# Softmax cross entropy on one core: labels' logits by a masked sum on VectorE instead of by gathers

## Chip, cores, metric

One core of one Trainium2 chip. The metric is device time in microseconds (us) of one execution; lower is better. All runs told of here are fast, with a granted clock of 1.00. When two kernels are compared as a ratio, it is the mean time of one kernel's fast runs over that of the other's fast runs of the same rounds, so it is not quite the ratio of the medians quoted beside it.

## The reference

```python
batch, seq, vocab = 16, 512, 32000        # logits float32, labels int
logits_max = np.max(logits, axis=-1, keepdims=True)
log_sum_exp = np.log(np.sum(np.exp(logits - logits_max), axis=-1)) + logits_max.squeeze(-1)
log_probs = logits - log_sum_exp[..., np.newaxis]
loss = -log_probs[np.arange(batch)[:, None], np.arange(seq), labels]
```

There are 8192 rows of 32000 logits, 1048.6 MB, each read once. A row needs the sum of its exponentials and one single element, its label's logit.

## The kernel before

The rows are laid over 128 partitions in 64 groups (`G`). A group is read in two loads of 16000 columns (8.19 MB each) into three buffers of 64 KB per partition. ScalarE takes exp in place and sums it in the same call (`accum_out`; the trace has one activation of 13.54 us and one accumulator read of 0.19 us for each). The labels' logits come from 64 gathers that GpSimd issues at the start, each fetching 128 single elements.

```python
    nc.gpsimd.iota(idx[:], pattern=[[V, G]], base=0, channel_multiplier=G * V)
    nc.gpsimd.tensor_tensor(out=idx[:], in0=idx[:], in1=labs32, op=ALU.add)
    for g in range(G):
        nc.gpsimd.indirect_dma_start(
            out=lab_logit[:, g:g + 1], out_offset=None, in_=lg,
            in_offset=bass.IndirectOffsetOnAxis(ap=idx[:, g:g + 1], axis=1),
        )
    # ...
    for j, (g, b, at, n) in enumerate(loads):
        if b not in buffers:
            buffers[b] = data.tile([P, W], FP32, tag="t", name="t")     # 3 buffers, W = 16000
        t = buffers[b]
        # ...
        nc.sync.dma_start(out=t[:, at:at + n], in_=lg_pg[:, g, c0:c0 + n])
        exp(g, t[:, at:at + n])          # one activation with accum_out
        # ... at the end: log of the sums, minus lab_logit, two small stores
```

The softmax here doesn't subtract the row's maximum and nothing guards it: scores larger than these inputs give would overflow.

Of the kernel before, what the change touches and what calls it, by code (L numbers as in the profile page):

```python
# [1 line left out]

# [5 lines left out]

FP32 = mybir.dt.float32  # L10
I32 = mybir.dt.int32


EXP = mybir.ActivationFunctionType.Exp
LN = mybir.ActivationFunctionType.Ln
ALU = mybir.AluOpType
X = mybir.AxisListType.X


@with_exitstack  # L20
def kernel(
    ctx: ExitStack,
    tc: tile.TileContext,
    logits: bass.AP,
    labels: bass.AP,
    out: bass.AP,
):
    nc = tc.nc

    B, S, V = logits.shape  # L30
    P = 128
    G = B * S // P
    W = 16000


    lg = logits.rearrange("b s v -> (b s) v")
    lg_pg = lg.rearrange("(p g) v -> p g v", g=G)
    labels_pg = labels.rearrange("b s -> (b s)").rearrange("(p g) -> p g", g=G)
    out_pg = out.rearrange("b s -> (b s)").rearrange("(p g) -> p g", g=G)



    loads = []

    def plan(g, widths_by_buffer, order):

        n_buffers = 1 + max((l[1] for l in loads), default=-1)
        for b, i in order:
            ws = widths_by_buffer[b]
            loads.append((g, n_buffers + b, sum(ws[:i]), ws[i]))  # L50

    plan(0, [[4000, 4000, 8000], [16000]], [(0, 0), (0, 1), (0, 2), (1, 0)])
    for g in range(1, G - 2):
        plan(g, [[W], [W]], [(0, 0), (1, 0)])
    plan(G - 2, [[W], [10000, 6000]], [(0, 0), (1, 0), (1, 1)])
    plan(
        G - 1,
        [[7400, 5840, 2260], [4540, 3720, 2920, 1780, 1460, 1120], [960]],
        [(0, 0), (0, 1), (1, 0), (1, 1), (1, 2), (0, 2), (1, 3), (1, 4), (1, 5), (2, 0)],
    )  # L60
    assert sum(l[3] for l in loads) == G * V

    data = ctx.enter_context(tc.tile_pool(name="data", bufs=3))
    persist = ctx.enter_context(tc.tile_pool(name="persist", bufs=1))

    labs64 = persist.tile([P, G], mybir.dt.int64)
    labs32 = labs64[:].bitcast(I32).rearrange("p (g two) -> p g two", two=2)[:, :, 0]
    idx = persist.tile([P, G], I32)
    lab_logit = persist.tile([P, G], FP32)
    K = 10  # L70
    sums = persist.tile([P, G - 1, 5], FP32)
    sums_last = persist.tile([P, K], FP32)
    totals = persist.tile([P, G - 1], FP32)
    logsum = persist.tile([P, G - 1], FP32)
    res = persist.tile([P, G - 1], FP32)
    part = persist.tile([P, 1], FP32)
    logsum_last = persist.tile([P, 1], FP32)
    res_last = persist.tile([P, 1], FP32)

    ctx.enter_context(tc.manual_schedule())  # L80


    nc.scalar.dma_start(out=labs64[:], in_=labels_pg)
    nc.scalar.preload_act_table_set("natural_log_exp_and_others")  # L84
    nc.vector.memset(sums[:], 0.0)  # L85
    nc.gpsimd.iota(idx[:], pattern=[[V, G]], base=0, channel_multiplier=G * V)  # L86
    nc.gpsimd.tensor_tensor(out=idx[:], in0=idx[:], in1=labs32, op=ALU.add)  # L87
    for g in range(G):
        nc.gpsimd.indirect_dma_start(  # L89
            out=lab_logit[:, g:g + 1],  # L90
            out_offset=None,
            in_=lg,
            in_offset=bass.IndirectOffsetOnAxis(ap=idx[:, g:g + 1], axis=1),
        )


    buffers = {}
    col = {}
    n_exp = {}

    def exp(g, ap):
        k = n_exp.get(g, 0)
        n_exp[g] = k + 1
        s = sums[:, g, k:k + 1] if g < G - 1 else sums_last[:, k:k + 1]
        nc.scalar.activation(out=ap, in_=ap, func=EXP, accum_out=s)  # L105

    for j, (g, b, at, n) in enumerate(loads):
        if b not in buffers:
            buffers[b] = data.tile([P, W], FP32, tag="t", name="t")
        t = buffers[b]  # L110
        c0 = col.get(g, 0)
        col[g] = c0 + n
        nc.sync.dma_start(out=t[:, at:at + n], in_=lg_pg[:, g, c0:c0 + n])  # L113
        exp(g, t[:, at:at + n])

        left = len(loads) - 1 - j
        if left == 6:
            nc.vector.reduce_sum(out=totals[:], in_=sums[:], axis=X)  # L118
        if left == 4:
            nc.scalar.activation(out=logsum[:], in_=totals[:], func=LN)  # L120
            nc.vector.tensor_tensor(out=res[:], in0=logsum[:], in1=lab_logit[:, 0:G - 1], op=ALU.subtract)  # L121
        if left == 1:
            nc.vector.reduce_sum(out=part[:], in_=sums_last[:, 0:K - 1], axis=X)  # L123
    assert n_exp[G - 1] == K
    nc.sync.dma_start(out=out_pg[:, 0:G - 1], in_=res[:])

    nc.scalar.activation(out=logsum_last[:], in_=sums_last[:, K - 1:K], func=LN, bias=part[:])  # L127
    nc.vector.tensor_tensor(out=res_last[:], in0=logsum_last[:], in1=lab_logit[:, G - 1:G], op=ALU.subtract)  # L128
    nc.sync.dma_start(out=out_pg[:, G - 1:G], in_=res_last[:])


# [1 line left out]
_INS = ['logits', 'labels']  # L133
_OUTS = [((16, 512), 'float32')]


# [23 lines left out]
```

## Time and profile before

| | before |
|---|---|
| time, median of 3 runs | 2435.72 us (2435.60 to 2435.73) |
| span in the profile | 2434.1 us |
| DMA rate over the span | 431 GB/s |
| ScalarE / VectorE busy | 72% / 0% |
| time between landings of two full loads, from 300 us on | 18.90 us |

These lines are from the page of the kernel before: the span, the busy time of each engine, the rate in 40 slices, the DMA queues (q1 carries the 1048.62 MB of the loads, q0 the gathers), the chain of work that ended last, two groups of instructions (busy us, mean ns | idle before) and the time from a load's issue to its landing.

```profile
span 2434.1 us, 807 instructions
...
DVE 1.3 (0%) x5; ACT 1748.9 (72%) x281; POOL 61.0 (3%) x70
...
GB/s 421 422 421 433 425 438 431 427 438 438 433 426 436 438 434 426 435 438 434 426 435 436 435 430 431 436 435 430 431 436 438 431 427 436 438 433 426 438 433 377
...
q1 hardware_dynamic: 20304, 1048.62, 99.8%
q0 software_dynamic: 2048, 0.04, 0.1%
...
q14 instruction: 6, 0.05, 0.0%
...
DMA t<-in_logits_dram 76%; ACT t L105 24%; SPq L113 0%; ACTq L105 0%; ACT logsum_last L127 0%; DVE res_last L128 0%; ACT logsum L120 0%
...
L105 ACT ACTIVATE t<-t 128x16000 f32<-128x16000 f32 (+5 forms) x139 | 1734.8, 12481 | 681.4 <-DMA t<-in_logits_dram 681.2
L89 POOL DMA_INDIRECT lab_logit<-in_logits_dram,idx x64 | 60.3, 942 | 178.3 <-DMA lab_logit<-in_logits_dram,idx 174.5
...
t<-in_logits_dram SPq DMA_DIRECT2D x124, 8000.0 KB, 43.0
```

The kernel is bound by its loads. ScalarE waits for landings (681 us in all); an exp holds up only the issue of a later load. The 24% of exp in the chain is not lost time: a load is issued when the exp three loads earlier frees its buffer (SyncE waits 2330.9 us for exps, 125 times), and its 43.0 us to the landing are 2.3 times the 18.90 us between landings, so it lies queued behind two others for most of them.

The windows of the kernel before (window, its length, busy time of VectorE, ScalarE and GpSimd with instruction counts, clock, DMA share, GB/s) show where the rate is lower:

```profile
60.00:120.00 60.00, 0.00 (x0) 41.67 (x7) 13.15 (x14) 1.00 1.01 427
...
180.00:240.00 60.00, 0.00 (x0) 43.35 (x7) 13.14 (x14) 1.00 1.01 427
...
600.00:1200.00 600.00, 0.00 (x0) 430.90 (x64) 0.00 (x0) 1.00 1.00 434
```

While GpSimd issues gathers, the loads run at 427 GB/s; afterwards at 434.

### The profile page before, as it was taken

How to read it: one execution, taken by the hardware profiler on the slowest of the kernel's cores; microseconds unless marked ns; L12 is line 12 of the kernel's file. 1: busy time of each engine (PE TensorE's matmuls, PEld its weight loads, DVE VectorE, ACT ScalarE, POOL GpSimd, SP SyncE). 2: the span in 40 equal slices, each digit the busy share in tenths (PEclk: the TensorE clock that was granted, in tenths of full speed). 3: DMA queues.
4: the chain of work that ended last, by engine and by line, in shares of the span. 5: the costliest groups of instructions: out<-in, count | busy, mean ns of one | idle time of the engine just before them, and what ended most of it. 6: DMA issues, size and time to landing. Idle time of an engine off the chain costs nothing.

```text
span 2434.1 us, 807 instructions
## 1 busy us (share of the span) xinstructions
DVE 1.3 (0%) x5; ACT 1748.9 (72%) x281; POOL 61.0 (3%) x70
## 2 busy tenths in 40 slices
DVE  0000000000000000000000000000000000000000
ACT  4777766777677776777677776777667776777769
POOL 3222000000000000000000000000000000000000
DMA  9999999999999999999999999999999999999998
GB/s 421 422 421 433 425 438 431 427 438 438 433 426 436 438 434 426 435 438 434 426 435 436 435 430 431 436 435 430 431 436 438 431 427 436 438 433 426 438 433 377
DMA packets 22502, 1048.77 MB, mean 431 GB/s; under 512 B 4576, under 2 KB 4704, under 8 KB 5216
## 3 DMA queue, kind: packets, MB, share of 16 engines
q1 hardware_dynamic: 20304, 1048.62, 99.8%
q0 software_dynamic: 2048, 0.04, 0.1%
q10 hardware_dynamic: 144, 0.07, 0.0%
q14 instruction: 6, 0.05, 0.0%
HBM read 1048.67 MB, written 0.03 MB: 431 GB/s over the span
## 4 chain that ended last, share of the span: by engine, by line
DMA 76%; ACT 24%; issue 0%; SPq 0%; ACTq 0%; DVE 0%
DMA t<-in_logits_dram 76%; ACT t L105 24%; SPq L113 0%; ACTq L105 0%; ACT logsum_last L127 0%; DVE res_last L128 0%; ACT logsum L120 0%
## 5 line engine op out<-in xcount | busy, mean ns | idle before, releaser
L105 ACT ACTIVATE t<-t 128x16000 f32<-128x16000 f32 (+5 forms) x139 | 1734.8, 12481 | 681.4 <-DMA t<-in_logits_dram 681.2
L89 POOL DMA_INDIRECT lab_logit<-in_logits_dram,idx x64 | 60.3, 942 | 178.3 <-DMA lab_logit<-in_logits_dram,idx 174.5
L105 ACT ACTIVATION_READ_ACCUMULATOR t<-t 128x1 f32 x139 | 25.9, 186 | 0.0
L84 ACT ACT_TABLE_LOAD x1 | 1.3, 1283 | 1.2 <-PEq L144 1.2
L118 DVE TENSOR_REDUCE totals<-sums 128x63 f32<-128x315 f32 x1 | 0.5, 480 | 2398.9 <-ACT t L105 2398.9
L87 POOL TENSOR_TENSOR idx<-idx,labs 128x64 int32<-128x64 int32 x1 | 0.3, 322 | 7.5 <-DMA labs<-in_labels_dram 7.5
L85 DVE MEMSET sums<- 128x315 f32 x1 | 0.3, 321 | 0.9 <-PEq L144 0.9
L127 ACT ACTIVATE logsum_last<-sums_last,part 128x1 f32<-128x1 f32 x1 | 0.3, 294 | 0.0
L121 DVE TENSOR_TENSOR res<-logsum,lab_logit 128x63 f32<-128x63 f32 x1 | 0.2, 225 | 25.3 <-ACT logsum L120 25.3
L120 ACT ACTIVATE logsum<-totals 128x63 f32<-128x63 f32 x1 | 0.2, 238 | 0.0
L86 POOL IOTA idx<- 128x64 int32 x1 | 0.2, 172 | 0.4 <-PEq L155 0.4
L123 DVE TENSOR_REDUCE part<-sums_last 128x1 f32<-128x9 f32 x1 | 0.2, 163 | 4.0 <-ACT t L105 4.0
L128 DVE TENSOR_TENSOR res_last<-logsum_last,lab_logit 128x1 f32<-128x1 f32 x1 | 0.2, 159 | 1.2 <-ACT logsum_last L127 1.2
L144 POOL MEMSET const-uint8-127<- 128x1 uint8 x1 | 0.1, 118 | 0.0
L144 POOL MEMSET const-bfloat16-1.0<- 128x1 bf16 x1 | 0.1, 113 | 0.0
L144 POOL MEMSET const-float32-0.0<- 128x1 f32 x1 | 0.1, 98 | 0.2 <-issue 0.2
L144 POOL MEMSET const-float32-1.0<- 128x1 f32 x1 | 0.1, 104 | 0.0
## 6 DMA issues: line engine op xcount, KB each, us to landing
t<-in_logits_dram SPq DMA_DIRECT2D x124, 8000.0 KB, 43.0
t<-in_logits_dram SPq DMA_DIRECT2D x1, 5000.0 KB, 35.9
t<-in_logits_dram SPq DMA_DIRECT2D x2, 2000.0 KB, 9.6
t<-in_logits_dram SPq DMA_DIRECT2D x1, 4000.0 KB, 21.4
t<-in_logits_dram SPq DMA_DIRECT2D x1, 3700.0 KB, 32.9
t<-in_logits_dram SPq DMA_DIRECT2D x1, 3000.0 KB, 42.6
t<-in_logits_dram SPq DMA_DIRECT2D x1, 2920.0 KB, 39.5
t<-in_logits_dram SPq DMA_DIRECT2D x1, 2270.0 KB, 26.4
```

The source lines that it names most:

```text
L84: nc.scalar.preload_act_table_set("natural_log_exp_and_others")
L85: nc.vector.memset(sums[:], 0.0)
L86: nc.gpsimd.iota(idx[:], pattern=[[V, G]], base=0, channel_multiplier=G * V)
L87: nc.gpsimd.tensor_tensor(out=idx[:], in0=idx[:], in1=labs32, op=ALU.add)
L89: nc.gpsimd.indirect_dma_start(out=lab_logit[:, g:g + 1], out_offset=None, in_=lg, in_offset=bass.IndirectOffsetOnAxis(ap=idx[:, g:g + 1], ...
L105: nc.scalar.activation(out=ap, in_=ap, func=EXP, accum_out=s)
L118: nc.vector.reduce_sum(out=totals[:], in_=sums[:], axis=X)
L120: nc.scalar.activation(out=logsum[:], in_=totals[:], func=LN)
L121: nc.vector.tensor_tensor(out=res[:], in0=logsum[:], in1=lab_logit[:, 0:G - 1], op=ALU.subtract)
L123: nc.vector.reduce_sum(out=part[:], in_=sums_last[:, 0:K - 1], axis=X)
L127: nc.scalar.activation(out=logsum_last[:], in_=sums_last[:, K - 1:K], func=LN, bias=part[:])
L144: nc = _bacc.Bacc("TRN2", target_bir_lowering=False, num_devices=1)
```

## The change

The intent is to take the 59 early gathers off the DMA and to use the idle VectorE: for each stretch of 4000 columns it multiplies the logits by (column number == label) and sums. The last five groups are still gathered. The exp of a full buffer is done in halves, so that the first half can start behind the first two masked sums.

```diff
+    H = 4000
+    NH = V // H
+    GG = G - 5
 ...
+    masked = psum.tile([P, H], FP32)
+    cols = persist.tile([P, H], mybir.dt.uint16)
+    lab_at = persist.tile([P, NH, G], FP32)
+    found = persist.tile([P, GG, NH], FP32)
 ...
-    for g in range(G):
+    for g in range(GG, G):
         nc.gpsimd.indirect_dma_start(
 ...
+    for h in range(NH):
+        nc.vector.tensor_scalar(
+            out=lab_at[:, h, :], in0=labs32, scalar1=float(-h * H), scalar2=None, op0=ALU.add
+        )
 ...
-        exp(g, t[:, at:at + n])
+        if g < GG:
+            for i in range(n // H):
+                h = c0 // H + i
+                lo = at + i * H
+                nc.vector.scalar_tensor_tensor(
+                    out=masked[:], in0=cols[:], scalar=lab_at[:, h, g:g + 1], in1=t[:, lo:lo + H],
+                    op0=ALU.is_equal, op1=ALU.mult, accum_out=found[:, g, h:h + 1],
+                )
+                if n == W and i % 2 == 1:
+                    exp(g, t[:, lo - H:lo + H])
+            if n < W:
+                exp(g, t[:, at:at + n])
+        else:
+            exp(g, t[:, at:at + n])
 ...
+            nc.vector.reduce_sum(out=lab_logit[:, 0:GG], in_=found[:], axis=X)
```

## The prediction

> **What bounds it now.** The loads. The page gives 1048.8 MB in a span of 2434.1 us, 431 GB/s, DMA busy 9 in every slice; ScalarE is busy 72%, VectorE 0%. The chain of waits is load, exp, load: 76% DMA, 24% exp. With three buffers, a load is issued when the exp of the load three earlier ends (13.64 us), and lands 43.0 us later, 2.3 times the pitch. In that chain the links repeat every 56.70 us, so one 8.19 MB load lands each 18.90 us, 433.4 GB/s[...]. Time can be won only where the loads run slower than that. While GpSimd issues its 64 gathers (9 to 247 us) the chain's links take 57.98, 57.88, 57.89 and 57.49 us: 4.4 us too much, during some 45 gathers, about 0.10 us each. Windows: 427 GB/s from 60 to 240 us, 434 after.
>
> **Removed.** 59 gathers. On the path only their disturbance of the loads counts: estimated 59 x 0.08 to 0.10 us, 5 to 6 us.
>
> **Added.** 472 masked sums of 128x4000 on VectorE. None is in the trace, so I estimate. The trace's VectorE operations in fp32[...] (128x315 reduce 480 ns, 128x63 tensor-tensor 225 ns, 128x1 159 ns). That gives 4.32 us, and an accumulator read of up to 0.16 us: 4.3 to 4.5 us, 17.3 to 18.0 us per load against 18.9. VectorE becomes 84 to 88% busy, and still keeps up. [...]
>
> **Moved.** exp of a full buffer becomes two of 8000 (6.87 us each, from the trace's own 128x8000), each behind two masked sums. ScalarE gains about 0.39 us per load, off the path (to about 74%). A buffer is held longer: four masked sums plus the last half, about 25 us after landing instead of 13.6. The next load into it is then issued about 31.7 us before it lands instead of 43: still 1.7 loads queued, so the longer hold costs nothing. The last five groups and the tail of small loads are unchanged.
>
> **Prediction: 2430.5 us**, 0.2% less; 8 in 10 within 2427 to 2441. Faster by over 2%: 1%. Within 2%: 92%. Slower by over 2%: 7%.
>
> **What would show it.** Right: masked sum 4.2 to 4.5 us; VectorE 84 to 88%; issue to landing near 32 us; links of the chain still 56.7 us for three loads, from the start on; rate near 433 GB/s in slices 2 to 4; saving made before 290 us, nothing after. Wrong, if issue to landing falls to about 21 us or less, with idle DMA slices, or if SyncE waits longest for masked sums.
>
> **What would make it wrong.** A masked sum over 4.72 us (a quarter of 18.9): VectorE sets the pitch, each further 0.1 us costing 118 x 0.4 = 47 us[...]. Or fewer queued loads let some DMA engines run empty: 0.3% of the rate lost would eat the whole gain. Or VectorE reading the buffers slows the DMA's writes. Or a gather costs less: 2435.

The sum came to 2435.7 us of the kernel before less 5.2 us for the 59 gathers, 2430.5 us. 4.32 us stands as the author's estimate from the three operations (redone below), and that nothing can be won below 18.90 us per load was the author's assumption; in the two traces no two full loads land closer than 18.88 us in mid-run (from 300 us on; worked out from the trace). The 21 us below which the queue was to run dry is an estimate as well: little more than one spacing of 18.90 us.

## More of the kernel before

The chain of waits of the kernel before, in order of time (start, length, what), has one more thing in it, which I did not follow up when I predicted:

```profile
1137.65 42.97 DMA t<-in_logits_dram
...
1194.35 43.65 DMA t<-in_logits_dram
...
1251.73 42.96 DMA t<-in_logits_dram
```

One load in mid-run takes 0.68 us longer than its neighbours, with no gather near. The same happens once more, to the load issued at 1988.81 us (43.62 us).

## The result

| | before | after |
|---|---|---|
| time, median (4 runs each, same rounds) | 2435.72 us (2435.60 to 2435.90) | 2437.39 us (2437.23 to 2437.58) |
| span in the profile | 2434.1 us | 2435.7 us |
| VectorE busy | 0% | 86% |
| issue to landing of a full load | 43.0 us | 31.7 us |

The ratio is 1.0007 with a 95% interval of 0.9989 to 1.0024. That interval holds 1, so it is "same"; but the two sets of runs do not overlap, and the traces account for the 1.6 us between the spans to a tenth of a us, as the table below shows.

The page of the changed kernel, the same lines (masked sums and their accumulator reads come in as groups of L133):

```profile
span 2435.7 us, 2052 instructions
...
DVE 2104.1 (86%) x958; ACT 1783.4 (73%) x515; POOL 16.1 (1%) x12
...
GB/s 422 436 432 427 436 437 436 424 435 437 435 431 429 436 436 434 428 434 436 435 430 430 437 437 433 426 435 437 435 429 431 436 437 433 427 436 434 436 428 338
...
q1 hardware_dynamic: 20304, 1048.62, 99.6%
q14 instruction: 15, 0.12, 0.0%
...
q0 software_dynamic: 160, 0.00, 0.0%
...
DMA t<-in_logits_dram 82%; DVE masked L133 15%; ACT t L120 2%; SPq L128 0%; DVEq L133 0%; ACT logsum_last L161 0%; DVE res_last L162 0%; ACT logsum L154 0%; ACTq L120 0%
...
L120 ACT ACTIVATE t<-t 128x8000 f32<-128x8000 f32 (+5 forms) x256 | 1758.6, 6869 | 648.5 <-issue 354.4
L133 DVE SCALAR_TENSOR_TENSOR masked<-cols,lab_at,t 128x4000 f32<-128x4000 uint16 x472 | 2073.8, 4394 | 149.4 <-DMA t<-in_logits_dram 137.0
...
L133 DVE DVE_READ_ACCUMULATOR masked<-cols,lab_at,t 128x1 f32 x472 | 66.9, 142 | 0.0
...
t<-in_logits_dram SPq DMA_DIRECT2D x124, 8000.0 KB, 31.7
```

VectorE keeps up: it still waits for loads (137 us), so the loads still set the pace. Queue q0 has shrunk from 2048 packets to 160. And q14, the queue labelled "instruction", has grown from 6 packets to 15. Now the chain of waits of the changed kernel around 390 us:

```profile
313.45 31.67 DMA t<-in_logits_dram
...
351.24 31.67 DMA t<-in_logits_dram
...
389.04 32.62 DMA t<-in_logits_dram
...
427.79 31.68 DMA t<-in_logits_dram
```

Every so often a load takes 0.95 us longer, and what it loses is not made up afterwards. The trace records sixteen completions for each load, and the engine that waits for the load starts only after the last of them: at load 121 of the changed kernel the first comes at 2233.3 us and the last at 2241.97 us, and VectorE, idle for 0.98 us by then, starts its next masked sum at 2242.06 us. Landing means the last of the sixteen here. Set beside each other, the landings of the same load in the two traces show when time was won and lost (counted from each span's start; worked out from the trace; the labels' load is counted as the first, so load 5 is the fourth load of logits):

```
load    landed before    after minus before
  5          42.1              -0.2
 21         349.0              -3.8
 25         424.6              -2.9     one step of about 0.97
 41         727.0              -2.0     another
 53         953.8              -1.0     another
 69        1256.9              -0.7     another, but before has one of 0.68 too
 81        1483.7              +0.3     another
 97        1786.1              +1.3     another
113        2089.1              +1.6     another, and before's second
129        2384.5              +1.6
```

Up to 349 us the change wins 3.8 us, with one step (at 137 us) already in it: the gathers were worth 4.8 us. Then it loses it again in steps. Eight steps in all, mean 0.965 us, cost 7.7 us; the kernel before has two of 0.67 us, 1.3 us, that do not show in the changed one. -4.8 + 7.7 - 1.3 = +1.6 us, which is the difference of the spans. This is bookkeeping within two traces; the experiments below test its parts. Between the steps the loads land 18.90 us apart in both kernels.

What happens at the steps? The trace of transfers has one of 8192 bytes on q14 about 16 us ahead of each: at 121.6, 387.2, 652.7, 937.2, 1202.8, 1468.4, 1734.0 and 2018.5 us. Most are 265.6 us apart, which is 14.05 loads. A load gives VectorE four masked sums, four accumulator reads and a wait, 9 instructions: 126 between two of these transfers (135 in the two cases where they are 284.5 us, 15.05 loads, apart). In the kernel before the two steps follow transfers 813 us apart, 43.0 loads, and ScalarE runs 3 instructions per load there (exp, accumulator read, wait): 129. So there is one such transfer for some 128 instructions of one engine's stream. The other q14 transfers in the changed kernel's mid-run, such as those at 227.6, 716.3, 1211.8, 1687.3 and 2179.4 us, come some 26 loads apart, which fits ScalarE's 5 instructions per load there (129), and the two at 719.6 and 1931.4 us are 64.1 loads apart, which fits SyncE's 2 (128); none of them is followed by a step of its own. With the label "instruction" I take each of these transfers for the fetch of such a block; the label, the 8192 bytes and the counts are what the traces show.

VectorE itself does not stall at such a transfer. Around 387.2 us its timeline has no gap; it idles longer than usual (1.94 us instead of 0.99) only later, for the load that is late:

```profile
387.32 0.14 DVE L133 DVE_READ_ACCUMULATOR masked<-cols,lab_at,t 128x1 f32 x1
387.49 4.39 DVE L133 SCALAR_TENSOR_TENSOR masked<-cols,lab_at,t 128x4000 f32<-128x4000 uint16 x1
...
402.86 4.39 DVE L133 SCALAR_TENSOR_TENSOR masked<-cols,lab_at,t 128x4000 f32<-128x4000 uint16 x1 [1.94 <-DMA t<-in_logits_dram]
```

The sixteen completions also show how such a step arises. The page counts 16 DMA engines; that each of a load's sixteen completions is that of one of them is my inference. For load 121, by how much the completions were ahead of the last one, in us (worked out from the trace; the last seven rows are the experiments' below):

```
                second last   third last   first
before              0.8          1.5        2.4
after               4.7          6.9        8.7
no_gather           0.3          1.6        2.5
long_reads          0.5          2.3        4.1
halves8000          1.7          3.1        5.2
tiny_vector         6.2          6.5        8.6
tiny_scalar         4.6          5.4        6.5
tiny_both           1.0          6.4        8.1
after_again         4.4          5.8        8.1
```

In the changed kernel one completion of sixteen falls behind by another 0.97 us at each step, until it is 4.7 us behind the second last and 8.7 behind the first. All loads then land at the time of that one.

In these two traces such a transfer cost time only where the completion that fell back was already the last, or nearly so. In the kernel before, ScalarE has a third transfer, at 371.5 us, 813 us ahead of the next, and no step follows it: the next load lands 18.93 us after its neighbour, 0.03 us late. Its completions fit one of them falling back from the middle into the last place, which it takes by that 0.03 us: the three that were last are now 0.03, 0.30 and 0.44 us ahead of it, and were 0, 0.27 and 0.41 us ahead of the last before. The next transfer of ScalarE, at 1184.9 us, then makes a step (worked out from the trace).

### The profile page after: what moved, and what is told of

It reads as the page before. It is cut to its first block, busy times and chain, and to the rows that moved or that the text cites. A ratio compares the mean times of both kernels' runs of the same rounds, so it can differ in the third digit from the quotient of the medians.

```text
span 2435.7 us, 2052 instructions
## 1 busy us (share of the span) xinstructions
DVE 2104.1 (86%) x958; ACT 1783.4 (73%) x515; POOL 16.1 (1%) x12
## 4 chain that ended last, share of the span: by engine, by line
DMA 82%; DVE 15%; ACT 2%; issue 1%; SPq 0%; DVEq 0%; ACTq 0%
DMA t<-in_logits_dram 82%; DVE masked L133 15%; ACT t L120 2%; SPq L128 0%; DVEq L133 0%; ACT logsum_last L161 0%; DVE res_last L162 0%; ACT logsum L154 0%; ACTq L120 0%
## 5 line engine op out<-in xcount | busy, mean ns | idle before, releaser
L120 ACT ACTIVATE t<-t 128x8000 f32<-128x8000 f32 (+5 forms) x256 | 1758.6, 6869 | 648.5 <-issue 354.4
L133 DVE SCALAR_TENSOR_TENSOR masked<-cols,lab_at,t 128x4000 f32<-128x4000 uint16 x472 | 2073.8, 4394 | 149.4 <-DMA t<-in_logits_dram 137.0
L133 DVE DVE_READ_ACCUMULATOR masked<-cols,lab_at,t 128x1 f32 x472 | 66.9, 142 | 0.0
L120 ACT ACTIVATION_READ_ACCUMULATOR t<-t 128x1 f32 x256 | 47.7, 186 | 0.0
L100 POOL DMA_INDIRECT lab_logit<-in_logits_dram,idx x5 | 12.1, 2428 | 1.8 <-issue 1.2
## 6 DMA issues: line engine op xcount, KB each, us to landing
t<-in_logits_dram SPq DMA_DIRECT2D x124, 8000.0 KB, 31.7
```

Source lines behind the costliest of these rows:

```text
L100: nc.gpsimd.indirect_dma_start(out=lab_logit[:, g:g + 1], out_offset=None, in_=lg, in_offset=bass.IndirectOffsetOnAxis(ap=idx[:, g - GG:g ...
L120: nc.scalar.activation(out=ap, in_=ap, func=EXP, accum_out=s)
L133: nc.vector.scalar_tensor_tensor(out=masked[:], in0=cols[:], scalar=lab_at[:, h, g:g + 1], in1=t[:, lo:lo + H], op0=ALU.is_equal, op1=ALU. ...
```

## Theories, and the experiments

Three suppositions, to be tested:

- **Fetch.** The loss is the fetching of VectorE's longer instruction stream. It goes through one of the sixteen DMA engines that also carry the loads, puts that one back by 0.97 us per block of 128 instructions, and each load lands with its slowest engine.
- **Queue.** The longer hold of a buffer leaves fewer loads queued (issue to landing 31.7 us instead of 43.0), so the DMA runs dry at moments.
- **Reads.** VectorE reading every buffer slows the DMA's writes into it.

The unbroken 18.90 us between the steps speaks against the last two already; the experiments make sure. They ran with runs of the kernel before: 2436.20 us (2435.79 to 2436.67, 9 runs) for the first four, 2436.10 us (2435.69 to 2436.61, 9 runs) for the last four. Each experiment was run five times.

### no_gather: the gathers' price alone

```diff
-    for g in range(G):
+    nc.vector.memset(lab_logit[:], 0.0)
+    for g in range(GG, G):          # GG = G - 5
         nc.gpsimd.indirect_dma_start(
```

> The kernel before with the 59 early gathers taken out and nothing put in their place (labels' logits of 59 groups stay 0, so the result is wrong on purpose). It measures the gathers' cost alone. From the landings of the changed kernel I read a gain of 4.8 us (3.84 us by the 21st load, with one step of 0.97 us already in it): all theories expect 2430.9 us, 4.8 under before. If it is under 1 us, the gathers never cost anything and the early gain comes from something else.

Measured: 2431.99 us (2431.59 to 2432.22), 4.2 us under before; ratio 0.9982, interval 0.9969 to 0.9996. The result is wrong. So 59 gathers cost 4.2 us, 0.07 us each; the first part of the change wins what the landings say, within 0.6 us.

### long_reads: same hold and much reading, few instructions

```diff
+            step = min(n, 8000)                        # on top of no_gather, for g < GG
+            for i in range(n // step):
+                lo = at + i * step
+                nc.vector.reduce_max(out=seen[:, 0:1], in_=t[:, lo:lo + step], axis=X)
+                exp(g, t[:, lo:lo + step])
```

> no_gather, plus two VectorE max-reductions of 128x8000 per full load and exp in halves behind them (result wrong on purpose). A buffer is held as long as in the changed kernel (about 24 us), VectorE reads as much of each buffer, the exp is as split, but VectorE has about 3 instructions per load instead of 9. Theory fetch (the loss is VectorE's instruction stream being fetched through the DMA engine that ends last, 0.97 us for each 128 instructions): 2 VectorE fetches in mid-run or 5 of ScalarE at 0.66, whichever DMA engine is more loaded: 2432 to 2433.5 us. Rival queue (a longer hold leaves fewer loads queued) and rival reads (VectorE's reading slows the writes of the DMA): as much lost as in the changed kernel, 6.5 us over no_gather: 2437.4 us.

Measured: 2433.08 us (2432.88 to 2433.62), 1.1 us over no_gather and 3.1 us under before; result wrong. Its page:

```profile
DVE 2004.3 (82%) x243; ACT 1783.4 (73%) x515; POOL 5.6 (0%) x11
...
q14 instruction: 10, 0.08, 0.0%
...
t<-in_logits_dram SPq DMA_DIRECT2D x124, 8000.0 KB, 32.6
```

VectorE is busy 82% of the time, the exp is in the same halves, and a load is issued only 32.6 us before it lands, nearly as in the changed kernel (31.7). Yet the 6.5 us that queue and reads called for are not there. The rivals fall, as far as this run goes (the ratio to before, 0.9987, has an interval of 0.9974 to 1.0001, which just includes 1; the runs of long_reads, no_gather and before do not overlap). One thing is not matched: a max-reduction reads one source, the masked sum two. The next run leaves no reading to speak of and keeps the count.

### tiny_vector: many instructions, no work

```diff
+        for i in range(8 * n // W if g < GG else 0):
+            nc.vector.tensor_scalar(
+                out=tiny[:, i:i + 1], in0=t[:, at:at + 1], scalar1=0.0, scalar2=None, op0=ALU.mult
+            )
         exp(g, t[:, at:at + n])
```

> The kernel before, all 64 gathers kept, plus 8 VectorE instructions of one column for each full load (944 in all), as many as the masked sums and their accumulator reads, and almost no VectorE time; exp, hold and queue as before; result right. Theory fetch: 8 steps of 0.97 us in the landings about every 14 loads, and before's two ScalarE steps of 0.66 us hidden beside them: 2435.7 + 7.7 - 1.3 = 2442.1 us. Rivals queue and reads: no change, 2435.7.

Measured: 2442.01 us (2441.84 to 2442.66), 5.8 us over before; ratio 1.0024, interval 1.0010 to 1.0038. (6.4 us over before was expected; that the time itself was met to 0.1 us owes something to a before that came out 0.5 us slower.) From its page, and from its chain of waits:

```profile
DVE 70.2 (3%) x949; ACT 1748.8 (72%) x281; POOL 61.0 (2%) x70
...
q14 instruction: 14, 0.11, 0.0%
...
t<-in_logits_dram SPq DMA_DIRECT2D x124, 8000.0 KB, 42.3
```

```profile
630.01 42.29 DMA t<-in_logits_dram
...
686.71 43.24 DMA t<-in_logits_dram
...
744.36 42.32 DMA t<-in_logits_dram
```

VectorE works 3% of the time, and the queue is nearly as deep as before (42.3 us). The steps of about 0.96 us are there all the same, in the same rhythm as in the changed kernel (seven between loads 21 and 125, as there). The number of instructions brings them about, without the work.

### tiny_scalar and tiny_both: another engine's stream, and two at once

```diff
         exp(g, t[:, at:at + n])
+        for i in range(8 * n // W if g < GG else 0):
+            nc.scalar.activation(out=tiny_a[:, i:i + 1], in_=zero[:], func=EXP)
```

This is tiny_scalar; tiny_both has these and those of tiny_vector.

> The kernel before plus only the 8 small ScalarE activations per full load (944), VectorE left alone. ScalarE's stream is then fetched about 10 times instead of 3. Theory fetch: 7 to 8 more visible steps of 0.66 us: 4.5 to 5.5 us over before. Together with tiny_vector and tiny_both it says whether the two streams add up (no: both was 5.8 over before, vector alone 5.8). If it costs nothing, then only VectorE's stream is dear.

> tiny_vector, plus 8 ScalarE activations of one column behind each exp of a full load, so that ScalarE's stream too has about 11 instructions per load and is fetched about 10 times. Theory fetch, with the two streams on two different DMA engines[...]: the larger lag counts, not the sum; 8 x 0.97 = 7.7 against about 10 x 0.66 = 6.6, so about 2442 us, as tiny_vector. If both streams come through one DMA engine, or if every fetch stops all engines: the sum, 2435.7 + 7.7 + 5.3 = 2448.7 us. Rivals queue and reads: 2435.7.

Measured: tiny_scalar 2440.77 us (2440.57 to 2441.35), 4.7 us over before (ratio 1.0020, interval 1.0006 to 1.0033), with steps of 0.68 us. They come 13.0 loads apart, and ScalarE has 10 instructions per load in this trace (one fewer than expected): 130, again some 128. tiny_both 2442.03 us (2441.75 to 2442.57), 5.8 us over its before (1.0010 to 1.0038): the same as VectorE alone, although q14 carries 22 packets there instead of 14. The sum would have been 10.5 us. From the pages of tiny_scalar and of tiny_both:

```profile
DVE 1.4 (0%) x6; ACT 1836.7 (75%) x1225; POOL 61.2 (3%) x70
...
q14 instruction: 13, 0.11, 0.0%
```

```profile
DVE 70.2 (3%) x950; ACT 1836.7 (75%) x1225; POOL 61.2 (3%) x70
...
q14 instruction: 22, 0.18, 0.0%
```

So the two streams seem to hold back two different completions of the sixteen, and only the worse of the two counted (5.8 us over before, not 10.5). The completions fit that: in tiny_both the second last of sixteen is only 1.0 us ahead of the last, and the third 6.4: two stragglers. This would also be why ScalarE's five transfers in the changed kernel cost nothing: after the last four of them the second last completion falls back by 0.65 to 0.70 us (from loads 41, 67, 92 and 118 on; worked out from the trace), but the last stays the last and no step of its own follows.

### tiny_gpsimd: a third stream

```diff
+    for i in range(944):                      # behind the gathers
+        nc.gpsimd.tensor_scalar(
+            out=tiny[:, i % 8:i % 8 + 1], in0=zero[:], scalar1=0.0, scalar2=None, op0=ALU.mult
+        )
```

> The kernel before plus 944 GpSimd instructions of one column behind its gathers, waiting for nothing; result right. About 7 fetches of GpSimd's stream, in quick succession. Theory fetch, if it holds for any engine's stream: 7 steps of 0.66 to 0.97 us, less the 1.3 us that they hide: 3.5 to 5.5 us over before. If GpSimd's stream is fetched where there is slack: nothing.

Measured: 2439.07 us (2438.79 to 2439.34), 3.0 us over before, somewhat under the range expected; the ratio's interval (0.9998 to 1.0026) just includes 1, the runs do not overlap. The direction holds for a third engine. The trace misses the landing of every eighth load, so single steps cannot all be read, but the sum can: from 254 to 429 us, beside seven more q14 transfers (267.9 to 397.3 us), the landings fall 4.6 us behind those of the kernel before, some 0.66 us per transfer, and the two later steps of the kernel before no longer show, which leaves 3.2 us (worked out from the trace).

### after_again and halves8000: half as many instructions for the same work

The masked sums take 8000 columns. To make room, the column numbers move to PSUM and the unused products to SBUF.

```diff
-    H = 4000
+    H = 8000
-    masked = psum.tile([P, H], FP32)
-    cols = persist.tile([P, H], mybir.dt.uint16)
+    cols_words = psum.tile([P, H // 2], FP32)
+    cols = cols_words[:].bitcast(mybir.dt.uint16)
+    masked = persist.tile([P, H], mybir.dt.bfloat16)
 ...
+                exp(g, t[:, lo:lo + step])        # behind each masked sum of 8000
```

> The changed kernel itself, once more, as the yardstick for the next run on the same chip: 1.7 us over before, as recorded (2437.4 against 2435.7).

> The changed kernel with masked sums of 8000 columns instead of 4000 (236 instead of 472, each with one accumulator read; the column numbers move to PSUM and the discarded products to SBUF to make room). The same VectorE reading, the same hold (about 25 us), the right result, but about 5 VectorE instructions per load instead of 9, so a fetch each 25 loads: 4 or 5 steps of 0.97 us instead of 8. Theory fetch: 3 to 4 us under the changed kernel, so about 2 us under before (0.1%). Rivals queue and reads: as the changed kernel. If an instruction of 8000 takes clearly more than twice 4.39 us, it tells nothing.

Measured: after_again 2437.13 us (2436.99 to 2438.26), 1.0 us over before (1.7 expected; before itself came out 0.4 us higher). halves8000 2434.27 us (2433.82 to 2434.93), result right: 2.9 us under after_again and 1.8 us under before. Its page:

```profile
DVE 2026.8 (83%) x486; ACT 1783.4 (73%) x515; POOL 12.2 (1%) x12
...
q14 instruction: 12, 0.10, 0.0%
...
L139 DVE SCALAR_TENSOR_TENSOR masked<-cols_words,lab_at,t 128x8000 bf16<-128x8000 uint16 (+1 forms) x237 | 2018.2, 8516 | 223.6 <-DMA t<-in_logits_dram 219.4
...
t<-in_logits_dram SPq DMA_DIRECT2D x124, 8000.0 KB, 32.4
```

The reading is not quite the same: one of the two sources now comes from PSUM instead of SBUF. VectorE works nearly as long and the hold is nearly the same; there are half as many masked sums, four large steps (0.96 to 0.99 us) and one of 0.4 us instead of eight: 4.3 us in all, against 7.1 us in after_again (seven of 0.97 us and a first one of only 0.33), and the 2.9 us fit that. It beats both kernels. The ratio to before, 0.9992, has an interval of 0.9979 to 1.0006, so by that measure it is "same"; the runs do not overlap.

## Why the prediction was right or wrong

The time was inside the range (2427 to 2441) and "within 2%" held, but the sign was wrong: 5.2 us less was predicted, 1.7 us more was measured. That the time fell inside the range is luck: the room above 2435 us was left for a starved queue, slowed writes or VectorE setting the pitch, none of which happened, and the cost that was overlooked was small enough to fit into it.

- **Bound by loads; VectorE keeps up.** Right. The masked sum took 4.39 us plus 0.14 for the read (4.3 to 4.5 predicted), VectorE was 86% busy (84 to 88), and it still waited for loads. The estimate can be redone from the three operations that it names: 1.01 to 1.06 ns per element between neighbours and some 0.16 us besides give 4.2 to 4.4 us.
- **A masked sum at half the estimated rate.** Measured: 4.39 us for 4000 elements are 1.10 ns each, with one 16-bit and one fp32 source in SBUF. With one of the two sources in PSUM (halves8000) 8000 elements took 8.55 us, 1.07 ns each, and a max-reduction with a single fp32 source (long_reads) 8.49 us, 1.06 ns each (both worked out from the pages' groups, less the two of 4000).
- **The gathers' price, 5 to 6 us.** Nearly right: 4.8 us by the landings, 4.2 us by no_gather.
- **"The longer hold costs nothing."** Right: issue to landing was 31.7 us, as worked out, and long_reads shows a hold that long without the loss.
- **VectorE's reading might slow the DMA's writes.** Not seen: between the steps the loads land 18.90 us apart with VectorE at 0% and at 86%, and long_reads, with VectorE at 82%, took 1.1 us over no_gather, not the 6.5 us that this called for.
- **"Saving made before 290 us, nothing after."** This step failed. The sum had a term too few: eight times the loads fall back some 16 us after a transfer on q14. The some 1,060 instructions added to VectorE's stream (472 sums, 472 reads, a wait for each of 120 loads) came with eight such transfers and eight steps of 0.965 us, 7.7 us, less the 1.3 us of the two steps of the kernel before, which no longer show. tiny_vector shows that the count does it without the work. The clue was in the trace before: two loads in mid-run 0.68 us late with no gather near, and a line for queue 14 on the page.

Still open: why the loads fall back by 0.97 us after a transfer of 8 KB for VectorE, and by 0.68 us after one for ScalarE, when its own record lasts 0.31 to 0.33 us. The trace does not name the DMA engine of a transfer, so that one engine carries all of a stream's blocks is concluded from the sixteen completions and from tiny_both, not read off.

## What to carry to other kernels

In this kernel, which loads without a break from end to end, instructions had a price in DMA time even on an engine that is otherwise idle (tiny_vector: VectorE 3% busy, 5.8 us over before): 7.5 ns for one of VectorE (0.965 us over 128), 5.3 ns for one of ScalarE (0.68 over 128). So prefer few long instructions in such a kernel (halves8000: half as many masked sums, 2.9 us less). The prices of VectorE and ScalarE did not add up in tiny_both, and single blocks cost nothing while another completion was the last: what counted was the longest lag. When a trace has loads that are late by a fixed amount at regular distances, count how many instructions lie between them.
